# Scale and shift modulation of layer 0 on TensorE in four column tiles, with the second halves of the first projection behind the loop

## Chip, cores and metric

The kernel runs on one core of a Trainium2 chip as one launch. A core has five engines that run beside each other: TensorE (PE; its weight loads are listed apart as PEld), VectorE (DVE), ScalarE (ACT), GpSimd (POOL) and SyncE (SP), which here only starts DMAs. The metric is device time in microseconds (us), lower is better.

## What is computed

Two layers of a trunk for 640 tokens: 512 latent tokens, modulated by the vector `c`, and 128 context tokens, modulated by `c_ctx`. For this change only the head of layer 0 matters:

```python
def modulation(cvec, w_mod, b_mod):
    m = jax.nn.silu(cvec) @ w_mod + b_mod
    return jnp.split(m[:, None, :], N_MOD, axis=-1)

def trunk_layer(x, cvec, lw, layer, ctx):
    sh1, sc1, g1, sh2, sc2, g2 = modulation(cvec, lw['w_mod'], lw['b_mod'])
    h = rmsnorm(x, lw['g_mix']) * (1.0 + sc1) + sh1
    mixed, new_ctx = token_mixers(h, lw, layer, ctx)   # begins with h @ lw['w_in']
```

The model width is 1024, so each of the six modulation vectors is a product of 1024 by 1024, needed for both condition vectors. The first columns of `w_in` that the kernel takes are the 512 of the convolution group (`conv_u`), in four column blocks of 128.

## The kernel before

Activations lie with the features on the 128 partitions and the 640 tokens along the free axis, so 1024 features are eight *granules* k = 0..7. Every matrix product runs in three passes (`mm3`): each operand is split into a rounded part (`hh`) and a rest (`hl`), and the products high by high, high by low and low by high are summed (lines 246, 247 and 248). Tokens are taken in two halves, `HALF`: h = 0 is columns 0 to 383, h = 1 is 384 to 639. Weights stream in as 512 KB tiles and are split by ACT (line 194) and by POOL or DVE (line 195).

`start()` (from line 1187) is the head of layer 0:

- SP starts, in this order, the loads of eight x tiles, of two modulation tiles, of the four weight granules of the convolution group, and then of the other modulation tiles in a ring of ten slots. There are 16 modulation tiles of 512 KB: for each granule k one of the scale vector (SC1) and one of the shift vector (SH1). Tiles 10 and 11 wait until the two tiles of granule 0 have been used, tiles 12 to 15 for those of granules 1 and 2.
- ACT squares x (line 1230), TensorE sums the squares over partitions (1235), some pairs being added by POOL first (1232, `SUMS`), and ACT turns the sums into `rn` (339, 340).
- TensorE spreads the conditioning vector over all partitions (1223), ACT copies that into `cb` (1239, `CB`).
- `dots(k)` computes the scale and the shift of granule k for both vectors. By the letter in `MODS` a tile is handled on DVE (D, line 303: multiply and reduce, one instruction for each vector), on POOL with the sum on ACT (G, lines 1268 and 1309), or on TensorE (P, line 1262: 128 by 128 stationary blocks of the tile against two columns). There are 8 tiles D, 5 G and 3 P.
- `norm(k)` adds the bias to the shift (1277), forms the gain (1279), and computes x times gain times rn on DVE (1290) and then, with the shift, the high part on ACT (1292). `low(k)` computes the low part on DVE (1303).
- `conv(i, h, k)` adds granule k to column block i of half h: three matmuls. Inside the loop seven of the eight (i, h) pairs are done for each k; block 3 of h = 1 comes after the loop, since its PSUM bank holds `pm`, the results of the P tiles.
- After the loop `conv_evac` takes the projection out of PSUM (lines 516, 522, 525), and the convolution's 62 taps follow on DVE (lines 421 and 425).

The sequence on each engine is fixed at compile time by a list scheduler that goes by priority and its own estimate of readiness; at run time each engine goes through its list in order. The taps and the products of the next modulation vector of layer 0 (G1, 16 instructions at line 303) are background jobs of lower priority on DVE. G1's tiles are loaded into slots that the ring of `start()` uses first. After the convolution blocks TensorE goes on with the other projections (`in_v`, `mtile`), then with the attention units; their rotary embeddings need DVE (490, 491), and the first score matmuls of a unit stand at lines 758 to 760.

Of the kernel before, what the change touches and what calls it, by code (L numbers as in the profile page):

```python
# [9 lines left out]
F32 = mybir.dt.float32  # L10
# [46 lines left out]
B_AT, B_SIZE = _addresses([("na", 11264), ("da", 11264)])  # L57
MODS = "DDGDDGPPDDGPDGGD"
RATE = (2700,1000,700,900,440)
# [12 lines left out]
PACE = 1  # L72
LOWK = "DDDDDADD"
SUMS = "DDDG"
XPOS = 8
LEADF = (2,3,4,5,6,7)
YOUT = ((2,4,6,8),(2,4,6,8))
CB = "AAAA"
KINDS = ("D", "D")
# [5 lines left out]
class Builder:  # L85
# [90 lines left out]

# [1 line left out]
    def after(self, a, b):  # L178
# [17 lines left out]

# [1 line left out]
    def w_raw(self, n):  # L198
# [43 lines left out]

# [1 line left out]
    def mm3(self, out, a, b, start, stop):  # L244
# [52 lines left out]

# [1 line left out]
    def mod_load(self, l, j, slot):  # L299
# [19 lines left out]

# [1 line left out]
    def sumsq(self, m, h, eng):  # L321
# [74 lines left out]

# [1 line left out]
    def conv_g(self, c):  # L398
# [86 lines left out]

# [1 line left out]
    def rope(self, dst, src, t0, n, rows=slice(0, 128)):  # L487
# [6 lines left out]

# [1 line left out]
    def mtile(self, evac):  # L496
# [187 lines left out]

# [1 line left out]
    def turn(self, u):  # L686
# [261 lines left out]

# [1 line left out]
    def out_pieces(self, l, regs, ngran, mt, last=False):  # L950
# [101 lines left out]

# [1 line left out]
    def ff_lead(self, l):  # L1054
# [114 lines left out]

# [1 line left out]
    def lam(self, l):  # L1171
# [15 lines left out]
    def start(self):  # L1187
# [8 lines left out]
        ring += [self.R(r, a, 1024) for r, a in (("oa", 4096), ("ob", 0), ("ob", 4096))]  # L1196
        prod = [self.F("conv", 4096 * s, 1024) for s in range(2)]
        self.junk = self.F("mla", 0, 1024)
        js = [w * 8 + k for k in range(8) for w in (SC1, SH1)]
# [25 lines left out]
        ps = [self.gb[1][:, 0:NLAT], self.sb[0][:, 0:T - NLAT]]  # L1225
        first = 1 if SUMS[0] == "G" else 0
        bufs = [self.F(*p, T) for p in (("tmp", 0), ("tmp", 3072), ("mla", 6144), ("conv", 8192))]
        for k in range(8):
            sq = bufs[k % 4]
            nc.scalar.activation(sq, self.x[:, k], AF.Square)  # L1230
            if k % 2 and SUMS[k // 2] == "G":
                nc.gpsimd.tensor_tensor(out=sq, in0=bufs[k % 4 - 1], in1=sq, op=ALU.add)
            if k % 2 or SUMS[k // 2] != "G":
                for v, a, b in seq:
                    nc.tensor.matmul(ps[v], self.ones, sq[:, a:b], start=k == first, stop=k == 7)
# [9 lines left out]
        acc = [self.sb[0][:, 0:512], self.sb[0][:, 512:1024], self.sb[1][:, 0:512], self.sb[1][:, 512:1024]]  # L1245
        acb = [self.sb[2][:, 0:512], self.sb[2][:, 512:1024], self.gb[1], self.gb[0]]
        ws = [self.w_get(128) for _ in range(4)]

        def conv(i, h, k):
            ps = (acb if h else acc)[i]  # L1250
            t0, t1 = HALF[h]
            self.mm3(ps[:, 0:t1 - t0], (ws[i][0][:, k], ws[i][1][:, k]), (self.hh[:, k, t0:t1], self.hl[:, k, t0:t1]),
                     k == 0, k == 7)

        def dots(k):
            late = []
            for i in (2 * k, 2 * k + 1):
                w, j = ring[i % n], js[i]
                if MODS[i] == "P":
                    w = w.rearrange("p (a b) -> p a b", b=128)  # L1260
                    for kt in range(8):
                        nc.tensor.matmul(pm[:, i], w[:, kt], ct[:, kt], start=kt == 0, stop=kt == 7)
                elif MODS[i] == "D":
                    for v in range(2):
                        self.mod_dot(0, j, w, v)
                else:
                    for v in range(2):
                        nc.gpsimd.tensor_tensor(out=prod[v], in0=w, in1=self.cb[:, v], op=ALU.mult)
                        late.append((prod[v], self.mods[:, 0, v, j:j + 1]))
                if 2 <= i < 16 - n:  # L1270
                    self.mod_load(0, js[i + n], ring[i % n])
            return late

        def norm(k):
            i, j = 2 * k, 2 * k + 1
            m = self.mods[:, 0, :, js[j]]
            nc.vector.tensor_scalar(out=m, in0=pm[:, j] if MODS[j] == "P" else m, scalar1=self.col(0, C_BMOD + js[j]),
                                    scalar2=None, op0=ALU.add)
            nc.vector.tensor_scalar(out=self.gs[:, 0, :, k], in0=pm[:, i] if MODS[i] == "P" else self.mods[:, 0, :, js[i]],
                                    scalar1=self.col(0, C_GMIX + k), scalar2=gain[:, k:k + 1], op0=ALU.mult, op1=ALU.add)  # L1280
            t = bufs[2 * k % 4]
            if LOWK[k] != "D":
                xr = bufs[(2 * k + 1) % 4]
                nc.vector.tensor_tensor(out=xr, in0=self.x[:, k], in1=self.rn, op=ALU.mult)
            for v, a, b in seq:
                sh = self.mod(0, v, SH1)[:, k:k + 1]
                if LOWK[k] != "D":
                    nc.scalar.activation(t[:, a:b], xr[:, a:b], AF.Identity, bias=sh, scale=self.gs[:, 0, v, k:k + 1])
                    continue
# [3 lines left out]
            if LOWK[k] != "D":  # L1293
                nc.scalar.copy(self.hh[:, k], t)
            return t

        def low(k, t):
            if LOWK[k] != "D":
                (nc.gpsimd if LOWK[k] == "G" else nc.vector).tensor_tensor(out=self.hl[:, k], in0=t, in1=self.hh[:, k].bitcast(F32),
                                                                           op=ALU.subtract)  # L1300
                return
# [5 lines left out]
        def accs(late):  # L1307
            for p, out in late:
                nc.scalar.activation(p, p, AF.Copy, accum_out=out)

        accs(dots(0))
        self.w_cut()
        for i in range(2, n + 2):
            self.mod_load(0, js[i], ring[i % n])
        for k in range(8):
            t = norm(k)
            late = dots(k + 1) if k < 7 else []
            accs(late)
            low(k, t)
            if k < 7:  # L1320
                for h in range(2):
                    for i in range(4 - h):
                        conv(i, h, k)
        self.ng = L * NGRAN
# [18 lines left out]
        self.table(TABLE_LN)  # L1343
# [225 lines left out]
def _layout(a):  # L1569
# [65 lines left out]
    wmod = np.ascontiguousarray(wmod)  # L1635
    for i, kind in enumerate(MODS):
        if kind == "P":
            j = (SC1, SH1)[i % 2] * 8 + i // 2
            wmod[0, j] = a["w_mod"][0, :, j * 128:j * 128 + 128].reshape(8, 128, 128).transpose(1, 0, 2).reshape(128, 1024)
    pairs = lambda k: k[0].reshape(L, 2, 2, 128, 64).transpose(0, 2, 4, 1, 3).reshape(L, 128, 2, 128)  # L1640
# [38 lines left out]
```

## Time and profile before

| | us |
|---|---|
| median of 3 runs | 1753.44 (1752.63 to 1755.69) |
| span of the profiled execution | 1755.2 |
| the run that fits it, 0.5 around the span | 1755.69 |
| TensorE busy | 1644.1 (94%) |
| VectorE busy | 1182.6 (67%) |
| ScalarE busy | 747.9 (43%) |
| GpSimd busy | 696.0 (40%) |
| DMA over the span | 178 MB, mean 102 GB/s |

The busy time of an engine is the sum of its instructions. Shares are means over a span whose stages have different limits, so the stage around the change is read by itself. PEclk is the clock granted to TensorE as a share of 2.4 GHz.

### The profile page before, as it was taken

The numbers are of one execution on the slowest core, as the hardware profiler recorded it, in microseconds if no ns is written. First come the engines' busy times: TensorE is split into PE (matmuls) and PEld (weight loads), VectorE is DVE, ScalarE is ACT, GpSimd is POOL, SyncE is SP. The second block draws the span as 40 slices with busy tenths as digits, with TensorE's granted clock in tenths as the row PEclk, the third lists the DMA queues.
The fourth block names the chain that finished last, engine by engine and source line by source line (L and its number), as shares of the span: only waits on it lengthen the run. The fifth ranks groups of instructions, "written<-read, shape, count | busy, mean of one in ns | idle before, by whom it ended". The sixth has DMA issues, their size and how long they took to land. (4 is left out here: it accounts for less than half of the span.)

```text
span 1755.2 us, 28692 instructions
## 1 busy us (share of the span) xinstructions
PE 1644.1 (94%) x10992; PEld 1568.0 (89%) x10992; DVE 1182.6 (67%) x2252; ACT 747.9 (43%) x1666; POOL 696.0 (40%) x538
## 2 busy tenths in 40 slices
PE   4896999998889999999999989999989999999998
PEld 3795888777789999999999979787879999999997
DVE  7999539899898887877367943787784333333335
ACT  5432667745533332233244237767553223223332
POOL 3454524413444454445332454432244333333330
PEclk7997999999989999999999989999999999999999
DMA  7451244334155444443222322440113222222211
GB/s 285 152 160 44 74 108 96 95 108 144 40 193 170 151 157 146 163 148 122 72 81 60 86 72 73 113 103 20 37 37 97 78 79 73 73 74 83 73 61 61
DMA packets 62330, 178.25 MB, mean 102 GB/s; under 512 B 8656, under 2 KB 20048, under 8 KB 62192
## 3 DMA queue, kind: packets, MB, share of 16 engines
q1 hardware_dynamic: 61984, 176.14, 32.2%
q8 instruction: 86, 1.41, 0.3%
q14 instruction: 52, 0.43, 0.1%
q0 software_dynamic: 64, 0.14, 0.0%
q10 hardware_dynamic: 144, 0.13, 0.0%
HBM read 158.52 MB, written 3.83 MB: 92 GB/s over the span
## 5 line engine op out<-in xcount | busy, mean ns | idle before, releaser
L195 POOL TENSOR_TENSOR ra<-fa,ra 128x512 fp32r<-128x512 f32 (+1 forms) x239 | 353.6, 1492 | 492.7 <-ACT ra L194 480.6
L195 POOL TENSOR_TENSOR we<-fa,we 128x512 fp32r<-128x512 f32 x126 | 187.1, 1496 | 288.3 <-ACT we L194 266.7
L1079 DVE TENSOR_TENSOR fr<-fr 128x384 f32<-128x384 f32 (+1 forms) x128 | 102.0, 800 | 273.2 <-ACT or L1078 150.7
L194 ACT CAST ra<-fa 128x512 fp32r<-128x512 f32 (+1 forms) x240 | 147.0, 621 | 232.6 <-PE s L247 125.0
L247 PE MATMUL s<-ra 128*128 128x384 f32 (+2 forms) x696 | 215.6, 310 | 0.9 <-POOL ra L195 0.9
L246 PE MATMUL s<-ra 128*128 128x384 f32 (+2 forms) x696 | 215.8, 310 | 0.7 <-ACT fr L1077 0.6
L248 PE MATMUL s<-ra 128*128 128x384 f32 (+2 forms) x696 | 215.4, 310 | 0.0
L303 DVE CUSTOM_DVE_ANT_0 fa<-fa 128x1024 f32<-128x1024 f32 x116 | 178.8, 1541 | 0.2
L394 DVE SCALAR_TENSOR_TENSOR fa<-s,fa 128x128 f32<-128x128 f32 (+1 forms) x306 | 120.3, 429 | 73.3 <-PE s L248 73.3
L194 ACT CAST we<-fa 128x512 fp32r<-128x512 f32 x132 | 81.5, 620 | 187.8 <-PE s L247 141.3
L246 PE MATMUL g<-ra 128*128 128x256 f32 (+2 forms) x412 | 131.0, 318 | 6.3 <-DVE bt L491 2.4
L394 DVE SCALAR_TENSOR_TENSOR fa<-g,fa 128x128 f32<-128x128 f32 (+1 forms) x270 | 110.5, 440 | 38.3 <-PE g L248 37.1
L248 PE MATMUL g<-ra 128*128 128x256 f32 (+2 forms) x412 | 126.7, 308 | 8.3 <-POOL ra L195 8.3
L246 PEld LDWEIGHTS s<-ra 128*128 128x128 f32 x696 | 132.7, 191 | 1.5 <-ACT fr L1077 1.3
L247 PEld LDWEIGHTS s<-ra 128*128 128x128 f32 x696 | 132.8, 191 | 1.1 <-POOL ra L195 1.1
L425 DVE SCALAR_TENSOR_TENSOR fa<-fa 128x670 f32<-128x670 f32 x120 | 133.5, 1170 | 0.2
L248 PEld LDWEIGHTS s<-ra 128*128 128x128 f32 x696 | 132.5, 190 | 0.0
L247 PE MATMUL g<-ra 128*128 128x256 f32 (+2 forms) x412 | 126.4, 307 | 0.0
L247 PE MATMUL s<-ra,we 128*128 128x256 f32 (+1 forms) x368 | 114.9, 312 | 10.8 <-DVE ra L372 10.8
L699 PE MATMUL g<-at 128*128 128x128 f32 x848 | 117.9, 278 | 5.1 <-DVE fa L394 1.6
L699 PEld LDWEIGHTS g<-at 128*128 128x128 f32 x848 | 106.7, 192 | 11.0 <-ACT fa L941 2.8
L246 PE MATMUL g<-or,ra 128*128 128x384 f32 (+1 forms) x322 | 110.1, 342 | 5.7 <-DVE fa L394 4.5
(284 smaller groups left out, 4667.6 us busy)
## 6 DMA issues: line engine op xcount, KB each, us to landing
fa<-in_wg SPq DMA_DIRECT2D x187, 512.0 KB, 3.6
fa<-in_wmod SPq DMA_DIRECT2D x77, 512.0 KB, 3.7
at<-in_wmod SPq DMA_DIRECT2D x16, 512.0 KB, 5.5
ra<-ra SPq DMA_DIRECT2D x64, 96.0 KB, 2.2
ra<-ra SPq DMA_DIRECT2D x64, 80.0 KB, 2.2
fa<-in_nab SPq DMA_DIRECT2D x24, 192.0 KB, 3.7
fa<-in_xT SPq DMA_DIRECT2D x8, 320.0 KB, 6.1
os<-in_wmod SPq DMA_DIRECT2D x3, 512.0 KB, 10.2
```

The costliest lines, as they stand in the source:

```text
L194: nc.scalar.copy(hi, src)
L195: (lo_eng or nc.gpsimd).tensor_tensor(out=lo, in0=src, in1=hi.bitcast(F32), op=ALU.subtract)
L246: nc.tensor.matmul(out, a[0], b[0], start=start, stop=False)
L247: nc.tensor.matmul(out, a[0], b[1], start=False, stop=False)
L248: nc.tensor.matmul(out, a[1], b[0], start=False, stop=stop)
L303: self.nc.vector.tensor_tensor_reduce(out=self.junk, in0=slot, in1=self.cb[:, v], scale=1.0, scalar=0.0, op0=ALU.mult, op1=ALU.add, accum_ ...
L394: self.mark = nc.vector.scalar_tensor_tensor(out=xs, in0=ps[:, a - t0:b - t0], scalar=self.mod(l, v, which)[:, m:m + 1], in1=xs, op0=ALU.m ...
L425: nc.vector.scalar_tensor_tensor(out=y, in0=g[:, j:j + 670], scalar=dwh[:, c, j:j + 1], in1=y, op0=ALU.mult, op1=ALU.add)
L699: self.nc.tensor.matmul(u["o"], v[:, p * 128:p * 128 + 128] if v.shape[1] > 128 else v, u["pt"][:, b * 128:b * 128 + 128], start=b == 0, s ...
L1079: nc.vector.tensor_tensor(out=r, in0=r, in1=r, op=ALU.mult)
```

## The change

All sixteen tiles now go to TensorE, with the operands exchanged: the two condition columns of `ct` are stationary (128 by 2), and the 128 by 128 block of the tile is the moving operand. The eight blocks of a tile write to four groups of two PSUM rows, at partitions 0, 32, 64 and 96, two blocks in a row on top of each other: four column tiles of the array. ACT copies the 256 columns of both tiles to SBUF (`rows`), and `gather` multiplies them by `sel`, a 128 by 2 matrix with ones where the partition number modulo 32 is 0 or 1. That sums the four groups and turns the row into a column. The copies of `cb` and three of the four pair sums go to DVE. In the loop only h = 0 of the projection is left; h = 1 follows as a block of its own. The evacuation of h = 0 is issued before it.

```diff
-MODS = "DDGDDGPPDDGPDGGD"
-LOWK = "DDDDDADD"
-SUMS = "DDDG"
+SUMS = "VVVD"
-CB = "AAAA"
+CB = "DDDD"
...
+        nc.vector.tensor_reduce(out=sel, in_=self.ident.rearrange("p (g r) -> p r g", r=32)[:, 0:2], axis=AX.X, op=ALU.add)
...
-            if k % 2 and SUMS[k // 2] == "G":
-                nc.gpsimd.tensor_tensor(out=sq, in0=bufs[k % 4 - 1], in1=sq, op=ALU.add)
+            if k % 2 and SUMS[k // 2] == "V":
+                nc.vector.tensor_tensor(out=sq, in0=bufs[k % 4 - 1], in1=sq, op=ALU.add)
...
-        acb = [self.sb[2][:, 0:512], self.sb[2][:, 512:1024], self.gb[1], self.gb[0]]
+        acb = [self.gb[1], self.sb[2][:, 0:512], self.sb[2][:, 512:1024], self.gb[0]]
...
         def dots(k):
-            late = []
+
+            part = self.sb[2][:, 512 * (k % 2):512 * (k % 2) + 256]
             for i in (2 * k, 2 * k + 1):
-                w, j = ring[i % n], js[i]
-                if MODS[i] == "P":
...
+                w = ring[i % n].rearrange("p (a b) -> p a b", b=128)
+                c0 = 128 * (i % 2)
+                for kt in range(8):
+                    g = 32 * (kt % 4)
+                    nc.tensor.matmul(part[g:g + 2, c0:c0 + 128], ct[:, kt], w[:, kt], start=kt < 4, stop=kt > 3)
                 if 2 <= i < 16 - n:
                     self.mod_load(0, js[i + n], ring[i % n])
-            return late
+            nc.scalar.copy(rows[k % 2], part)
+
+        def gather(k):
+            for i in (2 * k, 2 * k + 1):
+                c0 = 128 * (i % 2)
+                nc.tensor.matmul(pm[:, i], rows[k % 2][:, c0:c0 + 128], sel, start=True, stop=True)
...
-        accs(dots(0))
+        dots(0)
         self.w_cut()
         for i in range(2, n + 2):
             self.mod_load(0, js[i], ring[i % n])
+        gather(0)
+        dots(1)
         for k in range(8):
             t = norm(k)
-            late = dots(k + 1) if k < 7 else []
-            accs(late)
+            if k < 7:
+                gather(k + 1)
+            if k < 6:
+                dots(k + 2)
             low(k, t)
-            if k < 7:
-                for h in range(2):
-                    for i in range(4 - h):
-                        conv(i, h, k)
+            for i in range(4):
+                conv(i, 0, k)
...
-        for h in range(2):
-            for i in range(4 - h):
-                conv(i, h, 7)
-        for k in range(8):
-            conv(3, 1, k)
+        self.table(TABLE_TANH)
+        evs = [self.conv_evac(0, i // 2, "ba"[i % 2]) for i in range(4)]
         for i in range(4):
+            evs[i](0, acc[i])
+        for i in range(4):
+            for k in range(8):
+                conv(i, 1, k)
             self.w_done()
-        self.table(TABLE_TANH)
-        for i in (0, 2, 1, 3):
-            for h in range(2):
-                self.conv_evac(0, i // 2, "ba"[i % 2])(h, (acb if h else acc)[i])
+            evs[i](1, acb[i])
         self.table(TABLE_LN)
```

The host lays out all sixteen tiles as the three P tiles were laid out before; the bytes loaded are the same.

## Rows read from the trace of the kernel before

**Rows 1.** Stretches: busy (x instructions) of PE, PEld, DVE, ACT, POOL; clock; DMA share; GB/s.
```profile
20.00:26.30 6.30, 0.00 (x0) 0.00 (x0) 6.30 (x8) 6.24 (x11) 3.03 (x2) 0.54 1.03 412
35.70:40.70 5.00, 5.00 (x18) 5.00 (x19) 5.00 (x12) 1.47 (x3) 0.00 (x0) 0.50 0.29 93
...
13.20:77.70 64.50, 41.87 (x229) 36.48 (x228) 63.55 (x87) 29.14 (x55) 32.12 (x22) 0.81 0.58 217
...
82.60:140.00 57.40, 57.37 (x423) 57.17 (x422) 57.40 (x63) 17.11 (x40) 30.78 (x18) 1.00 0.48 149
140.00:182.00 42.00, 24.72 (x146) 22.83 (x144) 41.63 (x61) 8.98 (x23) 19.33 (x16) 0.76 0.19 56
```
**Rows 2.** VectorE's groups from 13.2 to 77.7 us: busy, mean ns, idle before.
```profile
L303 DVE CUSTOM_DVE_ANT_0 fa<-at,fa 128x1024 f32<-128x1024 f32 x8 | 11.0, 1372 | 6.2 <-DMA at<-in_wmod 6.1
...
L1277 DVE TENSOR_SCALAR fa<-fa 128x2 f32<-128x2 f32 x6 | 8.6, 1428 | 0.0
L303 DVE CUSTOM_DVE_ANT_0 fa<-os,fa 128x1024 f32<-128x1024 f32 x4 | 6.4, 1600 | 0.0
L195 DVE TENSOR_TENSOR ra<-os,ra 128x512 fp32r<-128x512 f32 x2 | 5.6, 2824 | 0.0
L303 DVE CUSTOM_DVE_ANT_0 fa<-fa 128x1024 f32<-128x1024 f32 x4 | 4.9, 1217 | 0.0
...
L195 DVE TENSOR_TENSOR wes<-fa,wes 128x512 fp32r<-128x512 f32 x4 | 2.5, 687 | 0.0
```
**Rows 3.** TensorE's groups from 26.3 to 82.9 us: the one with the longest idle time.
```profile
L247 PE MATMUL s<-ra,wes 128*128 128x384 f32 (+1 forms) x32 | 11.9, 373 | 11.7 <-DVE ra L1303 9.7 <-DVE ra L1299 2.0
```
**Rows 4.** Timeline of VectorE and ScalarE: start, duration, operation, idle before and releaser.
```profile
13.21 1.23 DVE L303 CUSTOM_DVE_ANT_0 fa<-at,fa 128x1024 f32<-128x1024 f32 x1 [6.06 <-DMA at<-in_wmod]
...
18.43 0.69 ACT L339 ACTIVATE fa<-g,fa 128x512 f32<-128x512 f32 x1 [3.51 <-PE g L1235]
...
38.45 1.01 DVE L1290 SCALAR_TENSOR_TENSOR fa<-fa 128x512 f32<-128x512 f32 x2
...
80.00 1.22 DVE L303 CUSTOM_DVE_ANT_0 fa<-at,fa 128x1024 f32<-128x1024 f32 x1
...
124.25 38.64 DVE L425 SCALAR_TENSOR_TENSOR fa<-fa 128x670 f32<-128x670 f32 x36
```
**Rows 5.** Timeline of TensorE: matmuls and one weight load.
```profile
36.51 0.53 PE L246 MATMUL s<-ra,wes 128*128 128x384 f32 x1
36.51 0.33 PEld L247 LDWEIGHTS s<-ra,wes 128*128 128x128 f32 x1
...
38.75 0.53 PE L248 MATMUL s<-ra 128*128 128x384 f32 x1
...
142.49 0.34 PE L247 MATMUL g<-ra 128*128 128x384 f32 x1
...
146.13 0.33 PE L247 MATMUL g<-ra 128*128 128x384 f32 x1
...
147.66 0.28 PE L247 MATMUL g<-ra 128*128 128x256 f32 x1
...
150.16 0.28 PE L247 MATMUL g<-ra 128*128 128x256 f32 x1
...
205.07 0.83 PE L699 MATMUL g<-at 128*128 128x128 f32 x6
...
208.83 0.39 PE L699 MATMUL g<-at 128*128 128x128 f32 x2
209.15 0.48 PE L758 MATMUL s<-bt 64*128 64x128 f32 x2
```
**Rows 6.** TensorE's groups by shape, whole span: the 128-column transposes of the first microseconds.
```profile
L1223 PE MATMUL s<-fa 128*128 128x128 f32 x16 | 3.7, 424 | 5.5 <-DVE fa L1184 5.5
```
**Rows 7.** Waits from 140 to 182 us: total, times, longest.
```profile
PE s L758 <- DVE fa L491: 14.1, 1, 14.1
```
**Rows 8.** VectorE's groups from 78 to 182 us: the products of vector G1.
```profile
L303 DVE CUSTOM_DVE_ANT_0 fa<-at,fa 128x1024 f32<-128x1024 f32 x16 | 24.9, 1557 | 0.0
```

More of the change, by code (lines that the diff above doesn't have):

```diff
@@ L1196, in start @@
         ring += [self.R(r, a, 1024) for r, a in (("oa", 4096), ("ob", 0), ("ob", 4096))]
-        prod = [self.F("conv", 4096 * s, 1024) for s in range(2)]
-        self.junk = self.F("mla", 0, 1024)
+        rows = [self.F("conv", 1024 * s, 256) for s in range(2)]
+        sel = self.F("conv", 2048, 2)
         js = [w * 8 + k for k in range(8) for w in (SC1, SH1)]
@@ L1225, in start @@
         ps = [self.gb[1][:, 0:NLAT], self.sb[0][:, 0:T - NLAT]]
-        first = 1 if SUMS[0] == "G" else 0
+        first = 0 if SUMS[0] == "D" else 1
         bufs = [self.F(*p, T) for p in (("tmp", 0), ("tmp", 3072), ("mla", 6144), ("conv", 8192))]
@@ L1230, in start @@
             nc.scalar.activation(sq, self.x[:, k], AF.Square)
[L1231 to L1233 removed]
+            if k % 2 and SUMS[k // 2] == "V":
+                nc.vector.tensor_tensor(out=sq, in0=bufs[k % 4 - 1], in1=sq, op=ALU.add)
+            if k % 2 or SUMS[k // 2] == "D":
                 for v, a, b in seq:
@@ L1255, in dots @@
         def dots(k):
-            late = []
+            part = self.sb[2][:, 512 * (k % 2):512 * (k % 2) + 256]
             for i in (2 * k, 2 * k + 1):
-                w, j = ring[i % n], js[i]
-                if MODS[i] == "P":
[L1260 to L1269, printed above, removed]
+                w = ring[i % n].rearrange("p (a b) -> p a b", b=128)
[3 more added lines that the diff above has]
+                    nc.tensor.matmul(part[g:g + 2, c0:c0 + 128], ct[:, kt], w[:, kt], start=kt < 4, stop=kt > 3)
                 if 2 <= i < 16 - n:
                     self.mod_load(0, js[i + n], ring[i % n])
-            return late
+            nc.scalar.copy(rows[k % 2], part)
[3 more added lines that the diff above has]
+                nc.tensor.matmul(pm[:, i], rows[k % 2][:, c0:c0 + 128], sel, start=True, stop=True)
         def norm(k):
@@ L1276, in norm @@
             m = self.mods[:, 0, :, js[j]]
[L1277 to L1284, printed above, removed]
+            nc.vector.tensor_scalar(out=m, in0=pm[:, j], scalar1=self.col(0, C_BMOD + js[j]), scalar2=None, op0=ALU.add)
+            nc.vector.tensor_scalar(out=self.gs[:, 0, :, k], in0=pm[:, i], scalar1=self.col(0, C_GMIX + k),
+                                    scalar2=gain[:, k:k + 1], op0=ALU.mult, op1=ALU.add)
+            t = bufs[k % 4]
             for v, a, b in seq:
                 sh = self.mod(0, v, SH1)[:, k:k + 1]
-                if LOWK[k] != "D":
-                    nc.scalar.activation(t[:, a:b], xr[:, a:b], AF.Identity, bias=sh, scale=self.gs[:, 0, v, k:k + 1])
-                    continue
                 nc.vector.scalar_tensor_tensor(out=t[:, a:b], in0=self.x[:, k, a:b], scalar=self.gs[:, 0, v, k:k + 1],
@@ L1292, in norm @@
                 nc.scalar.activation(self.hh[:, k, a:b], t[:, a:b], AF.Identity, bias=sh)
-            if LOWK[k] != "D":
-                nc.scalar.copy(self.hh[:, k], t)
             return t
         def low(k, t):
[L1298 to L1301, printed above, removed]
             for v, a, b in seq:
@@ L1305, in low @@
                                                in1=self.hh[:, k, a:b].bitcast(F32), op0=ALU.add, op1=ALU.subtract)
-        def accs(late):
-            for p, out in late:
-                nc.scalar.activation(p, p, AF.Copy, accum_out=out)
-        accs(dots(0))
+        dots(0)
         self.w_cut()
@@ L1635, in _layout @@
     wmod = np.ascontiguousarray(wmod)
[L1636 to L1639, printed above, removed]
+    for j in (*range(SC1 * 8, SC1 * 8 + 8), *range(SH1 * 8, SH1 * 8 + 8)):
+        wmod[0, j] = a["w_mod"][0, :, j * 128:j * 128 + 128].reshape(8, 128, 128).transpose(1, 0, 2).reshape(128, 1024)
     pairs = lambda k: k[0].reshape(L, 2, 2, 128, 64).transpose(0, 2, 4, 1, 3).reshape(L, 128, 2, 128)
```

## The prediction

> **What bounds the kernel now.** The page says TensorE 94% busy, but that is a mean, so I read the stretches first [rows 1]. From 13.2 to 77.7 us VectorE works 63.55 of 64.50 us and TensorE 41.87: the granule loop is bound by VectorE. TensorE's own groups confirm it: the second pass of the projection idles 11.7 us, nearly all of it for the low part of line 1303 [rows 3]. From 82.6 to 140 both engines are full (57.40 and 57.37 of 57.40). From 140 to 182 VectorE is full again (41.63 of 42.00) and TensorE has 24.72; in one piece it waits 14.1 us for a rotary product that stands behind a block of 36 taps of 38.64 us [rows 4, 7]. So two bounds matter: when TensorE ends the convolution columns (82.6), and when VectorE is free for its background work (77.7; its first G1 product starts at 80.00 [rows 4]). From 80 to 182 VectorE has no hole, so the second decides what is left of the gain at 182. Behind that TensorE is the bound and a shift stays.
>
> What fills VectorE in the loop [rows 2]: sixteen products of line 303 (11.0 + 6.4 + 4.9 = 22.3 us), and operations stretched far beyond their size. A 128x2 addition takes 1428 ns on average, and the same 128x512 split 2824 ns in one place and 687 in another. GpSimd is busy 32.12 us in this stretch [rows 1]; its 128x1024 products run at these places, and I put the stretching down to the two engines being in each other's way. That is read from coincidence in time.
>
> **Part 1: the products leave VectorE and GpSimd.** Away go the 22.3 us and all 128x1024 products of GpSimd, and with them most of the stretching. What stays on VectorE after 13.2 us: for each of 8 granules two pairs of 512 + 128 columns at 1.01 [rows 4] (the low pair has the same shapes) and two 128x2 operations, 0.5 together (my estimate), so 2.5, or 20 for eight; and seven weight splits at 0.69 [rows 2], 4.8. That is 25 instead of 63.55. The pair sums and `cb` copies that VectorE takes over (three of 640 columns, four of 512, at most 0.7 each by the 687 ns row: 5 us) lie before 16 us, where its first product waits for a tile until 13.21 [rows 4]: nothing. If that cover went, 5 us would come at the head, where x and the tiles still arrive, so at most 2 would show.
>
> **Part 2: the sum of squares.** ScalarE waits 3.51 us for the last sum, until 18.43 [rows 4]; the last pair was added on GpSimd before, and now each of its two squares goes straight to TensorE. I count 2 us earlier, bounds 0 and 3.5. What is late next are the tiles.
>
> **Part 3: the tiles.** Their bytes and order stay. Up to 26.3 us the transfers are saturated (share 1.03, 412 GB/s [rows 1]), so a tile of 0.524 MB takes 1.27 us. Tile 0 is there at 13.2 [rows 4], tile 1 at 14.5, the four weight granules by 19.6, tile 5 at 24.7, tile 15 at 37.4. Before, the last tiles came late because their slots were held (from 35.7 to 40.7 only 93 GB/s were moved [rows 1]). Now a slot is free when TensorE has read it, and SP, which waits in order, gets past. The weights, constants and bias tables queued behind land earlier, never later.
>
> **Part 4: TensorE in the loop.** Its order is dots(2), conv(0), gather(1 or 2), dots(3), and so on, so conv(0) starts behind tile 5: 24.7. Per granule:
> - `conv` h = 0: 12 matmuls of 384 columns. Their spacing at full clock is (146.13 - 142.49)/21 = 0.173, so 2.1 us; at half clock (38.75 - 36.51)/7 = 0.32, so 3.8 [rows 5].
> - `dots`: 16 matmuls with 128 moving columns. A plain fp32 one costs (0.83 - 0.39)/4 = 0.11 at 205 us [rows 5], and 3.7/16 = 0.23 in the first microseconds [rows 6], twice as much, so I take the head to run at 1.2 GHz. No row has column tiles. Lower end: four beside each other, 0.45. Upper end: each by itself with its whole duration, 0.424 [rows 6], 6.8. In between: one after another but overlapped, 1.8. I take 0.9, as the tiles use different columns of the array but every matmul also has a load of its own.
> - `gather`: two matmuls of two columns, at most 0.2; ScalarE's copy of 256 columns is below the 0.69 of 512 [rows 4] and lies two granules ahead.
> - Two changes of tile shape. Going from 128*128 to 64*128 at 209 us, the start comes at 209.15 where the spacing would give 208.83 + 0.22 = 209.05: 0.1 each [rows 5].
>
> The Trainium skill ("TensorEngine Tiling (Array Packing)", Key Properties) says that changing the tiling mode drains TensorE, which speaks against this change. The row agrees and prices it at 0.1; for the 16 changes it is 1.6 us of the loop, and they are in the sum.
>
> Sum: 0.9 + 0.2 + 0.2 + 2.1 = 3.4 at full clock, 6.2 at half. TensorE granted 0.50 while it ran densely from 35.7 to 40.7 [rows 1], so I let granule 0 and half of granule 1 run at half clock: 6.2 + 4.8, then 4 x 3.4, then two without dots 2 x 2.4. 24.7 + 11.0 + 13.6 + 4.8 = 54.1. VectorE ends one pair earlier, at about 53 (its own work from 17, 25, and 4 for waits on ScalarE, an estimate of 0.5 a granule, would let it end at 46, so TensorE sets it).
>
> **Part 5: the second halves.** 96 matmuls of 256 columns at (150.16 - 147.66)/21 = 0.119 [rows 5]: 11.4 us, ending at 65.5 instead of 82.6: 17 earlier. They were inside the loop before, in TensorE's idle time, so part of the gain goes back here. They cover the evacuation of h = 0, and the next granule's split. If that split came late, the cost is at most the longest one of the loop, 2.8 us [rows 2], once.
>
> **Part 6: what is left at 182.** TensorE alone would be there 17 us earlier. VectorE is free 77.7 - 53 = 25 us earlier, and whether it uses that depends on G1: 16 products of 24.9 us [rows 8], whose slots become free as dots(6) ends. Taps for the first channel block follow once its two halves are out, 5.7 us before the end of Part 5. If VectorE fills the gap, the whole chain from 80 to 182 moves by 25, and TensorE (65.5 + 57.4 + 24.7 = 147.6, against VectorE's 157) stays ahead of it; if it doesn't, by 17. I take 23, since G1 tiles need a few microseconds to land. Against the profiled execution's own time, 1755.7 for a span of 1755.2, that gives 1732.7; this run was the longest of three, and against the median of 1753.4 it is **1730**.
>
> **Rivals.**
> - A, column tiles one after another. dots costs 1.8, at half clock 3.7, and the loop is TensorE's: 24.7 + 8.1 + 6 + 4 x 4.3 + 4.8 = 60.8, end of Part 5 at 72.2, 10 earlier, VectorE free 18 earlier. About 14 us: 1739. For it: nothing in this trace runs two tiles side by side. Against: it needs no more than the ordinary overlap.
> - B, the other side: each small matmul waits for its own weight load and shows its whole duration, 0.42. Then a granule with dots costs 6.8 + 0.4 + 2.1 = 9.3, the loop ends at 24.7 + 6 x 9.3 + 4.8 = 85.3, Part 5 at 96.7, 14 later than before, and taps start at 91, about 10 later than the first G1 product did. With VectorE full up to 182 this costs 10 us: 1763. It decides from about 0.33 us a matmul (loop end 77, taps no earlier than 82.6). Against it: at 36.51 a weight load starts as the matmul before it starts and runs beside it for 0.33 us [rows 5], over all 128 rows. The Trainium skill ("TensorE: Matmul & The Clock Gate", Part 3, The mechanism) says that weight loads overlap a running matmul only where their row groups differ; all these matmuls use all four row groups, so by that sentence B would hold. The row contradicts it for whole-array tiles; no run here shows column tiles yet.
> - C, the change does little: dots at 0.3 a matmul, or a scheduler order in which convolution evacuations stand ahead of G1 and of the next splits so that the shift is eaten. 1752.
> - D, better than forecast: dots at 0.45, full clock from granule 1, and G1 filling all. VectorE free at 46 to 48, 30 to 32 us earlier: 1722.
>
> **How the numbers follow.** Forecast 0.55 (own range 1725 to 1736), A 0.22, D 0.12, C 0.05, B 0.06. A difference under 0.2% (3.5 us) can't be told from none here. Faster is the forecast, A and D, 0.89; same is C, 0.05; slower is B, 0.06. The range holds the forecast, all of D but its far tail and A with a margin for an order that eats some of it: 1717 to 1745; B and C lie outside.
>
> **What would show it.** Part 1: in the loop the VectorE pair at about 1.0 and no 128x2 operation over 0.5. Part 3: the last modulation tile landing near 37 us. Part 4: the spacing of the 128-column matmuls with two stationary columns, 0.03 to 0.06 for the forecast, 0.11 for A, 0.3 and more for B, and six granules of about 3.4 us. Part 5: the last 256-column matmul at about 65. Part 6: the first G1 product before 60, and the 14.1 us wait shorter or gone by the same shift. The prediction is wrong if dots costs over 2 us a granule, if TensorE stays at half clock through the loop, or if VectorE stands idle between its last low part and the first tap.

## The result, and the profile after

| | kernel before | changed kernel |
|---|---|---|
| median of 4 runs, us | 1753.04 (1751.6 to 1755.69) | 1743.24 (1740.93 to 1745.08) |
| ratio, 95% interval | 1 | 0.9937 (0.992 to 0.9954) |
| span of the profiled execution, us | 1755.2 | 1741.9 |

The change makes the kernel 0.63% faster, some 10 us by the medians and 13.3 by the two spans (the profiled run of the kernel before is the longest of its four). The forecast of 1730 asked for 23. The direction is right and 1743.24 lies in the range of 1717 to 1745, but by the medians less than half of the gain came. Line numbers of the helpers are 2 lower in the changed kernel (the projection is 244 to 246, taps 423, G1 products 301, rotary product 489, first scores 756); in `start()` the products are line 1262, the selection 1270, the pairs 1281 and 1288.

The stretches that answer to [rows 1], with the same columns:

```profile
20.00:26.30 6.30, 2.94 (x20) 1.55 (x21) 5.78 (x9) 3.88 (x8) 1.75 (x1) 0.50 1.02 409
35.70:40.70 5.00, 5.00 (x67) 3.66 (x56) 3.13 (x8) 1.77 (x4) 0.00 (x0) 1.00 0.99 368
13.20:77.70 64.50, 58.40 (x549) 47.33 (x548) 39.43 (x77) 23.70 (x48) 9.81 (x7) 0.89 0.65 240
82.60:140.00 57.40, 56.67 (x400) 55.62 (x399) 57.40 (x60) 16.20 (x40) 29.16 (x16) 1.00 0.43 129
140.00:182.00 42.00, 23.68 (x130) 21.78 (x131) 32.90 (x66) 12.19 (x32) 20.06 (x20) 0.72 0.14 42
```

The middle of the loop and the end of its last granule by themselves, in the changed kernel:

```profile
34.00:58.00 24.00, 24.00 (x262) 18.31 (x261) 14.34 (x36) 8.20 (x18) 0.42 (x2) 1.00 0.65 227
56.30:58.30 2.00, 2.00 (x14) 2.00 (x13) 1.47 (x4) 1.02 (x2) 0.00 (x0) 1.00 0.00 0
```

The loop has changed sides: from 13.2 to 77.7 TensorE is busy 58.40 us (41.87 before) and VectorE 39.43 (63.55 before), and from 34 to 58 TensorE has no gap. But from 140 to 182 TensorE does no more than before (23.68 against 24.72). The waits of TensorE from 58 to 192 us (line, what it waited for, total, times, longest) answer to [rows 7]:

```profile
PE s L756 <- DVE fa L489: 16.6, 1, 16.6
PE g L244 <- DVE bt L489: 2.4, 1, 2.4
```

The wait for the rotary product is still there, and it is longer than the 14.1 us before. VectorE's timeline (start, duration, operation) shows why, from its last low part to the end of the taps:

```profile
57.29 1.01 DVE L1288 SCALAR_TENSOR_TENSOR ra<-fa,ra 128x512 fp32r<-128x512 f32 x2 [0.53 <-ACT ra L1283]
59.81 1.72 DVE L520 SCALAR_TENSOR_TENSOR fa<-fa,s 128x384 f32<-128x384 f32 x2 [1.51 <-ACT fa L514]
...
62.58 0.16 DVE L1180 TENSOR_TENSOR fa<-fa 128x1 f32<-128x1 f32 x1 [1.01 <-ACT fa L1177]
...
64.95 0.39 DVE L520 SCALAR_TENSOR_TENSOR fa<-fa,s 128x128 f32<-128x128 f32 x1 [2.02 <-PE s L246]
...
65.50 0.63 DVE L419 TENSOR_SCALAR fa<-fa 128x670 f32<-128x670 f32 x1
66.04 1.22 DVE L301 CUSTOM_DVE_ANT_0 fa<-at,fa 128x1024 f32<-128x1024 f32 x1
...
68.02 2.32 DVE L301 CUSTOM_DVE_ANT_0 fa<-at,fa 128x1024 f32<-128x1024 f32 x1
...
112.38 41.74 DVE L423 SCALAR_TENSOR_TENSOR fa<-fa 128x670 f32<-128x670 f32 x39
```

The last low part in the kernel before, and then the score matmul that waits for the rotary product, in the kernel before (line 758 there) and in the changed one (line 756):

```profile
76.74 1.01 DVE L1303 SCALAR_TENSOR_TENSOR ra<-fa,ra 128x512 fp32r<-128x512 f32 x2 [0.40 <-ACT ra L1292]
```
```profile
164.66 0.77 PE L758 MATMUL s<-bt 64*128 64x128 f32 x2 [14.10 <-DVE fa L491]
```
```profile
155.89 0.76 PE L756 MATMUL s<-bt 64*128 64x128 f32 x2 [16.62 <-DVE fa L489]
```

VectorE's lead over the kernel before can be read at four places: 19.4 us at the last low part (58.3 against 77.7), 14.0 at the first G1 product (66.04 against 80.00 [rows 4]), 11.9 at the start of the long block of taps (112.38 against 124.25), and 8.8 at its end (154.12 against 162.89). TensorE's wait ends with the block: the score matmul starts at 155.89, 8.8 earlier than the 164.66 before. From there to the first normalisation matmul of the convolution (line 443; 190.2 before, 177.4 now) TensorE takes 21.5 us instead of 25.6, since two more waits of 1.7 and 0.6 us on ScalarE are gone there and less runs at the lower clock (by the mean granted clocks, 0.76 and 0.75, some 10 us instead of 13, an estimate). That makes 12.8, and it stays: from the second normalisation matmul (203.05 before, 190.0 now) to the end of the span it is 1552.2 us before and 1551.9 after.

### The profile page after: what moved, and what is told of

It is laid out like the page before. It is cut to its first block, busy times and chain, and to the rows that moved or that the text cites. A ratio compares the mean times of both kernels' runs of the same rounds, so it can differ in the third digit from the quotient of the medians.

```text
span 1741.9 us, 29105 instructions
## 1 busy us (share of the span) xinstructions
PE 1649.5 (95%) x11224; PEld 1570.2 (90%) x11224; DVE 1150.0 (66%) x2230; ACT 737.2 (42%) x1649; POOL 669.7 (38%) x527
## 4 chain that ended last, share of the span: by engine, by line
PE 68%; DVE 22%; issue 4%; ACT 3%; POOL 1%; DMA 0%; SPq 0%; DVEq 0%; ACTq 0%; POOLq 0%
PE s L245 13%; PE s L246 13%; PE s L244 13%; PE g L244 7%; DVE fa L423 7%; PE g L246 7%; PE g L245 7%; PE g L697 3%; DVE fa L301 2%; PE s L686 2%; DVE fa L392 2%; DVE ra L301 2%; DVE ra L370 1%; DVE fa L377 1%; DVE fa L870 1%
## 5 line engine op out<-in xcount | busy, mean ns | idle before, releaser
L245 PE MATMUL s<-ra 128*128 128x256 f32 (+2 forms) x704 | 219.5, 312 | 0.9 <-POOL ra L193 0.9
L244 PE MATMUL s<-ra 128*128 128x256 f32 (+2 forms) x704 | 219.6, 312 | 0.7 <-ACT fr L1075 0.6
L246 PE MATMUL s<-ra 128*128 128x256 f32 (+2 forms) x704 | 219.2, 311 | 0.0
L301 DVE CUSTOM_DVE_ANT_0 fa<-fa 128x1024 f32<-128x1024 f32 x112 | 173.6, 1550 | 0.2
L244 PEld LDWEIGHTS s<-ra 128*128 128x128 f32 x704 | 135.1, 192 | 2.1 <-ACT fr L1075 1.3
L245 PEld LDWEIGHTS s<-ra 128*128 128x128 f32 x704 | 135.2, 192 | 1.8 <-POOL ra L193 1.1
L246 PEld LDWEIGHTS s<-ra 128*128 128x128 f32 x704 | 135.0, 192 | 0.2 <-issue 0.2
L244 PE MATMUL g<-ra 128*128 128x256 f32 (+2 forms) x404 | 128.4, 318 | 4.9 <-DVE bt L489 2.4
L246 PE MATMUL g<-ra 128*128 128x256 f32 (+2 forms) x404 | 124.4, 308 | 8.3 <-POOL ra L193 8.3
L245 PE MATMUL g<-ra 128*128 128x256 f32 (+2 forms) x404 | 124.1, 307 | 0.0
```

The lines of the kernel that those rows point to most:

```text
L244: nc.tensor.matmul(out, a[0], b[0], start=start, stop=False)
L245: nc.tensor.matmul(out, a[0], b[1], start=False, stop=False)
L246: nc.tensor.matmul(out, a[1], b[0], start=False, stop=stop)
L301: self.nc.vector.tensor_tensor_reduce(out=self.junk, in0=slot, in1=self.cb[:, v], scale=1.0, scalar=0.0, op0=ALU.mult, op1=ALU.add, accum_ ...
```

## Experiments

The labels V and T in the expectations: V says that VectorE's background list sets the end of the head, T that the end follows TensorE's own order. For all kernels one table of what the traces show; a ratio is taken against runs of the kernel before beside them. "Copy" is the start of ScalarE's first copy of a value tile (128x256, line 569), which marks how far TensorE's list has come behind the projection of the convolution; "waits" are TensorE's from there to "norm", the first matmul of line 443; "rest" is what lies between them without the waits.

| kernel | copy | waits | rest | norm | span | ratio (95%) |
|---|---|---|---|---|---|---|
| before | 90.92 | 18.8 | 80.5 | 190.2 | 1755.2 | 1 |
| order_only | 97.69 | 16.1 | 77.4 | 191.2 | 1754.1 | 0.9993 (0.9983 to 1.0002) |
| changed | 79.63 | 19.0 | 78.8 | 177.4 | 1741.9 | 0.9937 (0.992 to 0.9954) |
| after_again | 80.84 | 19.6 | 77.7 | 178.1 | 1741.7 | 0.9931 (0.9914 to 0.9948) |
| serial | 92.26 | 9.4 | 78.3 | 180.0 | 1745.1 | 0.9939 (0.9926 to 0.9951) |
| half_dots | 76.44 | 19.2 | 78.7 | 174.3 | 1736.1 | 0.9916 (0.9904 to 0.9928) |
| g1_early | 85.86 | 11.8 | 77.9 | 175.6 | 1739.4 | 0.992 (0.9906 to 0.9933) |
| rope_first | 78.21 | 17.2 | 81.4 | 176.8 | 1744.6 | 0.9959 (0.9945 to 0.9972) |
| after_sum | 80.37 | 19.8 | 77.4 | 177.6 | 1744.2 | 0.9927 (0.9914 to 0.9941) |
| no_g1 | 77.75 | 13.8 | 77.6 | 169.2 | 1733.3 | 0.9897 (0.9881 to 0.9913) |
| no_g1_sum | 79.29 | 6.8 | 78.3 | 164.4 | 1728.4 | 0.9844 (0.983 to 0.9857) |
| short_list | 79.44 | 5.2 | 77.4 | 162.0 | 1726.9 | 0.9853 (0.9833 to 0.9872) |
| g1_tensor | 90.11 | 6.2 | 77.1 | 173.4 | 1739.6 | 0.9924 (0.9908 to 0.994) |
| g1_tensor_sum | 88.92 | 0 | 75.1 | 164.0 | 1729.5 | 0.9863 (0.985 to 0.9877) |

The rest is 77 to 81 us wherever TensorE waits, and 75.1 where it doesn't. It is a difference, so the columns add up by construction; what the table shows is that the rest stays within 6 us while the copy moves by 21 and the waits by 20. So "norm" is TensorE's position plus nearly one amount of work plus its waits, and what one engine gains can be lost in the wait for the other.

**order_only**: the kernel before with the new order of the projection alone.

```diff
-                for h in range(2):
-                    for i in range(4 - h):
-                        conv(i, h, k)
+            for i in range(4):
+                conv(i, 0, k)
...
+        for i in range(4):
+            for k in range(8):
+                conv(i, 1, k)
```

> The kernel before, with its modulation on VectorE and GpSimd, but with the second halves of the projection behind the granule loop and the evacuation order of the change. The 11.4 us of second halves leave TensorE's idle time, so the projection ends 8 to 11 us later than in the kernel before, at 91 to 94. Theory V: VectorE starts G1 at 77 to 80 as before and has 40 taps instead of 36 in the block; the wait at the score matmuls shrinks by what TensorE is late; 1752 to 1758. Theory T: 1761 to 1764.

1754.78 us, no different from before. TensorE's list came 6.8 us later (copy at 97.69), and its waits were 2.7 shorter. This is V's range, and V's 40 taps stand in the block; T asked for 1761 or more. The order by itself neither costs nor brings anything.

**serial**: the changed kernel with all eight blocks of a tile in one group of two rows, without column tiles; `sel` has its ones in the first two rows only, to fit.

```diff
...
-                    g = 32 * (kt % 4)
-                    nc.tensor.matmul(part[g:g + 2, c0:c0 + 128], ct[:, kt], w[:, kt], start=kt < 4, stop=kt > 3)
+                    nc.tensor.matmul(part[0:2, c0:c0 + 128], ct[:, kt], w[:, kt], start=kt == 0, stop=kt == 7)
```

> The changed kernel without column tiles: all eight blocks of a tile are summed in one group of two rows. If column tiles run beside each other, the 32 matmul records of a granule go from 0.034 us spacing to about 0.11 at full clock, 2.4 us a granule, and the projection ends 15 to 20 us later, at 86 to 91. Theory V: G1 fills VectorE's gaps in the longer loop, all taps then stand ahead of the rotary product, which comes at about 160 to 165, as before the change: 1749 to 1756. Theory T: the projection ends 4 to 8 us later than in the kernel before: 1757 to 1761.

1745.71 us, which can't be told from the changed kernel, and faster than both theories said (V 1749 to 1756, T 1757 to 1761). Two tiles on TensorE's timeline:

```profile
35.63 1.92 PE L1261 MATMUL s<-fa 128*2 128x128 f32 x16
37.38 1.91 PE L1261 MATMUL s<-os,fa 128*2 128x128 f32 x16
```

A tile takes (37.38 - 35.63)/16 = 0.11 us a record, as expected, three times what it takes with column tiles. TensorE's list is 12.6 us later at the copy, and all but 2.6 of it comes out of the wait (9.4 instead of 16.6 at line 756, and the 2.4 gone). So the 11.3 us by which the change brought TensorE's list forward are nearly worthless here: TensorE reaches the scores early and stands there.

**g1_early**: the first six G1 products stand ahead of the evacuation of the first halves.

```diff
...
+        for _, step, _ in self.g1[:6]:
+            step()
...
+            with self.tc.issue_after(self.dot.ins):
+                evs[i](0, acc[i])
...
```

> The changed kernel, but the first six G1 products stand in VectorE's list ahead of the evacuation of the first halves, in the gap that VectorE has between 58.3 and 65. The list then has 46 taps in the block ahead of the rotary product instead of 39. Theory V: the first G1 product starts at 54 to 60 instead of 66.04, the rotary product comes 1 to 4 us earlier, as most of the head start is spent on the seven more taps: 1739 to 1742. Theory T: TensorE's projection ends as before, 1742 to 1745.

1742.27 us, where V's range ends and T's begins, so the time doesn't choose between them. VectorE's first G1 product is at 58.38, as V said, but the evacuations now hold TensorE up (copy 6.2 us later), and the taps start at 76.43. The scores start at 154.70, 1.2 earlier. In this order the hole before G1 isn't had for nothing: what fills it delays what TensorE needs.

**rope_first**: the rotary product goes ahead of 22 taps (17 before it instead of 39).

```diff
...
+                if da and l == 0:
+                    self.fill(450)
...
+        if l == 0:
+            self.mark = self.roped
```

> The changed kernel, but the taps after about the 34th are tied behind the rotary products of the shared key in VectorE's list: 17 taps stand in the block ahead of them instead of 39. Theory V (VectorE's list bounds the head: what stands ahead of the rotary product sets the end, TensorE's lead is lost in the 16.6 us wait at 139): the score matmuls start near 139 to 141 instead of 155.9, the taps end some 5 us later, and the time falls by 8 to 15 us, to 1728 to 1735. Theory T (the end of TensorE's projection block sets the end; the waits behind it are alike in both kernels and cancel): the work that the wait let VectorE do comes due a little later, time 1741 to 1745.

1749.47 us, by the ratios 4 us behind the changed kernel (the intervals overlap), and neither theory has it. TensorE's waits in this kernel, 58 to 192 us:

```profile
PE g L443 <- POOL fa L438: 7.7, 1, 7.7
PE s L690 <- ACT fa L718: 4.5, 2, 3.8
PE g L244 <- DVE bt L489: 3.7, 2, 2.5
...
```

The score wait is gone and 17.2 us of others have come: the last tap ends at 175.3 instead of 166.5, and POOL's sum of the convolution (line 438) comes after it. Moving one instruction forward moves the wait.

**no_g1**: G1's products over 8 of 1024 columns. It asks what VectorE's list is worth.

```diff
+        n = 8 if l == 0 and j // 8 == G1 else 1024
...
-            out=self.junk, in0=slot, in1=self.cb[:, v], scale=1.0, scalar=0.0,
+            out=self.junk[:, 0:n], in0=slot[:, 0:n], in1=self.cb[:, v, 0:n], scale=1.0, scalar=0.0,
```

> Left out: 1016 of the 1024 columns of each of the 16 G1 products of layer 0 (their instructions, loads and waits stay), so VectorE loses 27.8 us less some 3 us of fixed costs. Theory V (VectorE's list from the first G1 product to the last tap, POOL's sum behind it and the two normalisation matmuls of the convolution set the end of the head; TensorE only waits there): first tap at about 65, last tap at 142 instead of 166.4, the marker (second normalisation matmul, 190.0 in the changed kernel) at 170 to 174, TensorE's 18 us of idle time in 140 to 180 gone, 1724 us (1720 to 1729). Theory T (the end follows TensorE's own order from the end of its projection block, which does not move): marker within 3 us of 190, 1740 to 1745.

1736.45 us: 7 less than the changed kernel, where V said 19 and T nothing. The last tap ended at 134.8, earlier than V had said, and still a wait was left. TensorE's wait, then POOL's timeline:

```profile
PE s L245 <- POOL ra L193: 13.8, 1, 13.8
```
```profile
110.83 3.29 POOL L193 TENSOR_TENSOR ra<-fa,ra 128x512 fp32r<-128x512 f32 x2 [3.75 <-ACT ra L192]
134.83 1.38 POOL L439 TENSOR_TENSOR fa<-fa 128x670 f32<-128x670 f32 x1 [20.72 <-DVE fa L424]
136.17 4.93 POOL L193 TENSOR_TENSOR ra<-fa,ra 128x512 fp32r<-128x512 f32 x4
```

POOL takes its list in order. It stood 20.72 us at the sum of the convolution (line 439 here), waiting for VectorE's last tap, and the weight splits that TensorE needed stood behind it. This gives theory W: the end of the head is TensorE's position plus its work plus its wait for whatever stands behind VectorE's taps, on VectorE or on POOL.

**short_list**: no_g1, and the 30 odd taps over 8 of 670 columns.

```diff
...
-            nc.vector.scalar_tensor_tensor(out=y, in0=g[:, j:j + 670], scalar=dwh[:, c, j:j + 1],
-                                           in1=y, op0=ALU.mult, op1=ALU.add)
+            n = 8 if l == 0 and j % 2 else 670
+            nc.vector.scalar_tensor_tensor(out=y[:, 0:n], in0=g[:, j:j + n], scalar=dwh[:, c, j:j + 1],
+                                           in1=y[:, 0:n], op0=ALU.mult, op1=ALU.add)
```

> Left out: as in the run without G1, and also all but 8 of the 670 columns of the 30 odd taps of the layer 0 convolution; VectorE's list is some 27 us shorter again (last tap near 115). Theory V: the bound passes from VectorE to TensorE here, because TensorE has only about 18 us of idle time between 60 and 205 to give; so this is within 4 us of the run without G1, 1718 to 1728. If VectorE still set the end, it would be another 25 us faster, 1699. Theory T: 1740 to 1745.

1728.72 us, just above V's range of 1718 to 1728: with the last tap at 111.1, 24 us earlier than in no_g1, 8 us are gained and not 25. TensorE is nearly the bound now; a last wait of 5.2 behind POOL's sum is left.

**g1_tensor**: the eight G1 tiles take the same way as the other sixteen, on TensorE.

```diff
...
+            if i:
+                late_gather(i - 1)
+            pair(acc[i], late[2 * i:2 * i + 2])
+            nc.scalar.copy(rows[i % 2], acc[i][:, 0:256])
...
-            self.bg = self.mod_jobs(0, [G1], [self.A("vb", 4096 * s, 1024) for s in range(3)], BGP[2], KINDS[0],
-                                    self.F("e", 4096, 1024)) + self.bg
...
```

> Nothing left out: the eight G1 tiles go the way of the scale and shift tiles, on TensorE in column tiles with a selection matmul, one pair behind each block of the second halves. VectorE loses 27.8 us and gets eight small operations; TensorE gets 8 x 0.55 us of products and 8 selection matmuls of 0.25 us and eight changes of tile shape, 6 to 8 us. Theory V: projection ends at 78 instead of 71.3, last tap near 142, marker at 174 to 180, 1729 us (1723 to 1735). Theory T: 6 to 8 us slower than the changed kernel, 1749 to 1752.

1741.41 us, against V's 1729 and T's 1749 to 1752. TensorE's list is 10.5 us later at the copy, more than the 6 to 8 expected (1.9 of it a selection's wait for VectorE, the second row), and the last tap ends at 139.5. The wait that is left stands behind the same sum on POOL:

```profile
PE s L245 <- POOL ra L193: 6.2, 1, 6.2
PE s L1333 <- DVE fa L1334: 1.9, 1, 1.9
```
```profile
139.54 1.38 POOL L438 TENSOR_TENSOR fa<-fa 128x670 f32<-128x670 f32 x1 [13.07 <-DVE fa L423]
140.88 4.94 POOL L193 TENSOR_TENSOR ra<-fa,ra 128x512 fp32r<-128x512 f32 x4
```

**after_again**, the control:

> The changed kernel itself once more, beside the others on the same chip: 1742 to 1745 by every theory, 9 to 13 us under the kernel before.

1743.79 us, as expected.

**half_dots**: the changed kernel with half of the products of each scale and shift tile.

```diff
-                for kt in range(8):
+                for kt in range(4):
...
-                    nc.tensor.matmul(part[g:g + 2, c0:c0 + 128], ct[:, kt], w[:, kt], start=kt < 4, stop=kt > 3)
+                    nc.tensor.matmul(part[g:g + 2, c0:c0 + 128], ct[:, kt], w[:, kt], start=kt < 4, stop=True)
```

> Left out: the second four of the eight products of each scale and shift tile, so 8 matmuls a granule stay of 16 (each leaves two records). Theory N (TensorE's own list paces the granule loop, and the products cost 1.1 us of each granule, not the 0.9 of the forecast): granule pace 4.1 down to 3.5 us, projection end 71.3 to 66 or 67, first G1 product 66.0 to 61 or 62, the second normalisation matmul 190.0 to 185 or 186, 1739 us (1736 to 1741). Theory L (the loop is paced by the chain of VectorE's and ScalarE's norm steps): pace and end within 1 us of the changed kernel, 1742 to 1745.

1741.83 us, between the ranges of N and L; the profiled run, of span 1736.1, is the fastest of five, and the ratio's interval overlaps that of the changed kernel, so the time shows no gain. In the trace the copy comes 3.2 us earlier, the scores 2.5 and "norm" 3.1, so N has the direction and not the size: it expected 4 to 5 and a pace of 3.5. The pace is as L said: the selections still follow each other by 4.1 us (54.02 - 37.72, by four). But L's reason isn't seen: TensorE is busy 24.00 of 24.00 us from 34 to 58 here too, as the scheduler filled the room with matmuls of the second halves. Tiles in the changed kernel and one here, on TensorE's timeline:

```profile
30.28 1.04 PE L1262 MATMUL s<-fa 128*2 128x128 f32 x16
...
33.12 0.62 PE L1262 MATMUL s<-fa 128*2 128x128 f32 x16
...
41.24 0.62 PE L1262 MATMUL s<-os,fa 128*2 128x128 f32 x16
41.79 0.45 PE L245 MATMUL s<-ra 128*128 128x384 f32 x1
...
42.42 0.59 PE L1270 MATMUL g<-fa 128*128 128x2 f32 x4
...
43.59 0.62 PE L1262 MATMUL s<-at,fa 128*2 128x128 f32 x16
...
45.38 0.62 PE L1262 MATMUL s<-at,fa 128*2 128x128 f32 x16
...
46.56 0.59 PE L1270 MATMUL g<-fa 128*128 128x2 f32 x4
```
```profile
42.94 0.40 PE L1262 MATMUL s<-at,fa 128*2 128x128 f32 x8
```

A tile leaves sixteen records, two for each of its eight matmuls; here eight, for four. Half of them cost 0.22 of 0.62 us, so 0.18 of each tile doesn't come from the number of matmuls.

**after_sum**: only the sum of the convolution goes to VectorE.

```diff
-        nc.gpsimd.tensor_tensor(out=ys, in0=y[0], in1=y[1], op=ALU.add)
+        (nc.gpsimd if l else nc.vector).tensor_tensor(out=ys, in0=y[0], in1=y[1], op=ALU.add)
```

> Only the sum of the two convolution halves of layer 0 moves from POOL to VectorE. In the changed kernel TensorE's wait is for a rotary product queued behind the taps on VectorE, and POOL's sum has nothing of TensorE's weights behind it. Theory W (the end of the head is the end of TensorE's projection, plus its work, plus the wait in which it stands for something behind VectorE's taps): same wait, 1742 to 1745. Theory P (POOL's queue is the wait's real cause): the 16.6 us wait shrinks by 3 us or more and the time falls below 1740.

1743.25 us with the same 16.6 us wait: in the changed kernel POOL's queue is not the cause.

**no_g1_sum**: the edits of no_g1 and of after_sum together.

> Left out: G1's products, as in the run without G1; and the convolution's sum of layer 0 moves from POOL to VectorE. In the run without G1 the wait left on TensorE was 13.8 us for a weight split that stood on POOL behind this sum, and so behind the last tap. Theory W: the 13.8 us wait goes or shrinks to 3 us or less (a rotary product behind the taps is next), second normalisation matmul 181.8 to 169 to 173, 1722 to 1727 us. Rival X (the wait only moves to the next product behind the last tap): wait over 10 us again, 1732 to 1737.

1728.47 us, 8 below no_g1 (9 by the ratios). The 13.8 us wait is gone, but 6.8 came in its place, for a rotary product on VectorE behind the taps. W and X each have half: the wait did move, at half the size.

**g1_tensor_sum**: the edits of g1_tensor and of after_sum together; nothing is left out.

> Nothing left out: G1 on TensorE as in the run before, and the convolution's sum of layer 0 on VectorE instead of POOL. There the last wait of TensorE was 6.2 us for a weight split on POOL behind this sum. Theory W: that wait goes, second normalisation matmul 186.0 to 180 or 181, 1735 us (1732 to 1738), faster than the changed kernel by 6 to 11 us. Rival X: the wait moves to the next product behind the last tap, 1740 to 1743.

1731.76 us (1731.51 to 1732.24), 0.9863 of the kernel before and so faster than it and than the changed kernel: 11.5 below after_sum, which ran beside it on the same chip and can't be told from the changed kernel; the intervals are well apart. It is even just below W's range of 1732 to 1738, and a second thing ends with the wait. The stretches of this kernel from the copy on, then those of the changed kernel around its wait, and one of g1_tensor behind its wait (136.0 to 142.2):

```profile
88.90:140.00 51.10, 51.10 (x371) 50.74 (x370) 50.73 (x42) 16.56 (x41) 25.15 (x17) 1.00 0.32 91
140.00:164.00 24.00, 24.00 (x157) 22.59 (x156) 12.80 (x37) 9.76 (x26) 16.27 (x18) 1.00 0.37 117
```
```profile
139.00:155.90 16.90, 0.28 (x4) 0.10 (x2) 16.48 (x24) 0.00 (x0) 1.07 (x2) 0.60 0.00 0
...
159.00:162.00 3.00, 2.06 (x6) 2.06 (x7) 3.00 (x7) 1.55 (x4) 2.32 (x3) 0.50 0.00 0
162.00:165.00 3.00, 3.00 (x11) 3.00 (x11) 2.96 (x6) 0.82 (x3) 3.00 (x3) 0.50 0.00 0
165.00:177.40 12.40, 12.40 (x81) 11.74 (x80) 4.85 (x18) 5.61 (x15) 8.68 (x10) 0.95 0.41 123
```
```profile
144.00:145.00 1.00, 1.00 (x6) 1.00 (x5) 0.00 (x0) 0.46 (x2) 1.00 (x2) 0.50 0.78 147
```

Without a wait TensorE is busy 75.1 of 75.1 us at a granted clock of 1.00. In the changed kernel it falls to 0.50 (1.2 GHz) while TensorE stands, and is still there 9 us after the wait. In g1_tensor the wait of 6.2 us was followed by 0.50 as well. From there to this kernel "norm" moves by 9.4 us: 6.2 are the wait, 2.0 the rest (77.1 to 75.1), and 1.2 an earlier copy.

## Why the prediction was off

- **Part 1** was right. With POOL nearly idle in the loop (0.42 us from 34 to 58) the 128x2 operations take 221 and 272 ns (1428 before [rows 2]) and a pair 1.01 to 1.02.
- **Part 2** was right: the logarithm starts at 15.47 instead of 18.43, 3 us for the forecast 2 and inside its bounds.
- **Part 3** was right: transfers are full up to 40.7 (0.99 and 368 GB/s in the second stretch above; 0.29 and 93 before), and in all TensorE waited 0.5 us for modulation tiles.
- **Part 4** had the form, TensorE setting the pace, and its terms were too small. The first projection matmul stood at 22.60, not behind tile 5 (24.7); it waited for ScalarE's high part (line 1283). Column tiles do lie beside each other: 0.034 us a record at full clock ((41.79 - 41.24)/16), at the lower end of the 0.03 to 0.06 that the prediction gave as its sign, where serial has 0.11. So A and B are out as mechanisms. But the prediction's rows count records, and each fp32 matmul leaves two, so a granule has 32 of them where it summed 16; and 0.18 us of each tile doesn't go with their number. The products of a granule cost 2 x 0.62 = 1.24 us for the 0.9 forecast, the selection 0.59 for 0.2. With the changes of shape the forecast was 0.9 + 0.2 + 0.2 = 1.3; the pace of 4.1 (selections at 42.42 and 46.56) less 2.1 for the projection leaves 2.0. The half speed ended near where it was put (24.7 + 6.2 + 3.1 = 34.0; the tile at 30.28 took 1.04, the one at 33.12 took 0.62), but by then granule 0 of the projection was done, where the forecast had half of granule 1 as well. VectorE was free at 58.3 instead of 53.
- **Part 5** has the right spacing (0.12 us a matmul), but TensorE's list behind the projection came 11.3 us earlier (copy at 79.63 for 90.92), not 17; what is missing is Part 4's.
- **Part 6 is the step that failed**: "I take 23, since G1 tiles need a few microseconds to land." It took VectorE to fill the gap and everything behind it to move rigidly. The tiles were not the matter: from 56.30 to 58.30 nothing was being transferred any more, and g1_early, which starts the same three loads at the same time (48.35 for 48.19), has its first G1 product at 58.38. VectorE stood 4.5 us in three waits between 58.3 and 65, because evacuations of the projection and the lambda scalars are fixed ahead of G1 in its list; this was the third condition under which the text called itself wrong. G1 then took 27.8 us for 24.9 [rows 8], and the scheduler set 39 taps for 36 ahead of the rotary product (41.74 for 38.64). So of the forecast's 24.7 us, 5.3 were gone when VectorE left the loop (Part 4), 5.4 by the first G1 product, 2.1 by the block of taps and 3.1 in it, which left 8.8 at the wait; the 4 us that TensorE saved behind it came on top. Part 6 also let TensorE come earlier ("stays ahead of it") and counted that as no loss: its lead only lengthened the wait.

G1's group in the changed kernel, and POOL's timeline at its start:

```profile
L301 DVE CUSTOM_DVE_ANT_0 fa<-at,fa 128x1024 f32<-128x1024 f32 x16 | 27.8, 1736 | 0.0
```
```profile
67.84 7.73 POOL L193 TENSOR_TENSOR ra<-fa,ra 128x512 fp32r<-128x512 f32 x4 [16.29 <-ACT ra L192]
```

Of the sixteen products eight took 1.9 to 2.3 us and the others 1.2; in the kernel before five took 2.3. Those three more make up the 2.9 us by which G1 grew. All the long ones overlap POOL's weight splits, though some of the short ones do as well.

That the time lies in the range at all is owed to the margin for an order that eats some of the gain, not to the forecast's sum. Rival A's number (1739) came nearer than the forecast, but for a reason that is not A's: serial has the products one after another, at A's 0.11 us a record, and its time can't be told from that of the changed kernel. C named the mechanism, an order in which evacuations stand ahead of G1, as one of its causes, and priced it at the whole gain; it took 5.4 us of VectorE's lead, from 19.4 to 14.0.

On the two rules that were weighed: the Trainium skill ("TensorE: Matmul & The Clock Gate", Part 3, The mechanism) has weight loads overlap only where the row groups differ, though a sentence before it also lets a load into the background weight buffer go ahead. The column tiles all use the same 128 rows and follow each other every 0.034 us, and the measurement decides. By the Trainium skill ("TensorEngine Tiling (Array Packing)", Key Properties) a change of tiling mode drains TensorE. The 0.18 us that half_dots leaves to each tile go with that; no run here separates the drain from the first load.

What stays open: why the scheduler put 39 taps ahead of the rotary product. Their number moves with the edits (36 before, 40 in order_only, 46 in g1_early, 55 in serial), and its estimates weren't varied by themselves.

## What to carry to other kernels

When two engines are each full in turn, follow the lead of each separately to the place where one waits for the other; only the smaller lead counts there, and the other turns into a longer wait. In a fixed list the work at the end of a chain can hold up an engine far from it: POOL's sum behind the last tap held weight splits that had nothing to do with it, and one line moved was worth 8 to 10 us once VectorE's list was short, and nothing before (after_sum). In these traces a wait of TensorE went with 2 us or more besides its length (the rest is 75.1 us without a wait, 77 to 81 with one), with the granted clock still at 0.50 behind it.

## What was not expected of the hardware

- An fp32 matmul leaves two records: 8 issued give x16, in 0.62 us at full clock; at half clock the same tile took 1.04.
- VectorE's G1 product took 1.22 us at 66.04, with POOL idle, and 2.32 at 68.02, while POOL split weights (67.84 to 75.57); so the stretching beside POOL, which Part 1 read from coincidence, is there in the background list too. It is a coincidence in time here as well: no run takes POOL's splits away by themselves.
- In all fourteen traces the second normalisation matmul stands 1549.2 to 1553.9 us ahead of the end, although it moves by 29 us: what is won in the head stays won.
